# Attention of a two-layer trunk: one group of steps per unit, latent values for both sample tiles at once, and TensorE's mixers in the order of the source

## The chip, the cores and the metric

The kernel runs on one core of a Trainium2 chip. The metric is the device time of one execution in microseconds (us); it was run three times. Engines: TensorE (PE; its weight loads are listed as PEld), VectorE (DVE), ScalarE (ACT), GpSimd (POOL) and SyncE (SP), whose queue starts most transfers.

## The reference

Two layers of a trunk for 128 prompt tokens and 256 sample tokens, which share all weights (fp32, width 1024). In each layer three mixers read the same normalised input; a merge of them goes through one output projection; a squared-ReLU MLP follows.

```python
h = rms(x) * (1 + sc1) + sh1                     # shift, scale, gate from the condition
u_conv, dq, dk, dv, cq, ckv, kpe, gl = split(h @ w_in)
o_conv = silu(rms(dwconv31(a * sigmoid(gate)))) @ w_conv_out
# differential: 4 heads, two 64-wide halves each, values 128 wide
q, k = rms64(dq), rms64(dk)                      # sample: 2-d rope, 128 cached keys in front
w = softmax(q1 k1 / 8) - lam * softmax(q2 k2 / 8)
o_diff = (rms128(w @ v) * (1 - lam_init)) @ w_diff_out
# latent: 8 heads, 96-wide queries and keys, values 64 wide
qm = rms96(rms(cq) @ w_uq);  k_nope, vm = split(rms(ckv) @ w_ukv)
km = rms96(k_nope ++ kpe)                        # rope on the last 32; cached ckv, kpe in front
o_mla = (softmax(qm km / sqrt(96)) @ vm) @ w_mla_out
x = x + g1 * ((s0 * o_conv + s1 * o_diff + s2 * o_mla) @ w_out)      # s = sigmoid(gl)
x = x + g2 * (relu(h2 @ w_up) ** 2 @ w_down)
```

The prompt attends to its own 128 keys; the sample to 128 cached and its own 256, 384 together.

## The kernel before

**Tokens and projections.** The 384 tokens are three tiles of 128 (tile 0 the prompt, tiles 1 and 2 the sample). Activations lie feature-major, 128 channels by 384 tokens. Every fp32 product with a weight is made from rounded parts: `split` (L194, L195) cuts a weight into a rounded `wh` (ScalarE) and the rest `wl` (VectorE), and `passes` (L201 to L203) issues three matmuls. A weight buffer comes free when its last matmul has run; `wh` has four, `wl` three, and the raw pieces `wr` four. The loads go through SyncE's queue in the order of use.

**The main line and its side lines.** `mixers` runs `weave(dense, chains, attention)`. `dense` is the main generator: the projections for differential attention (`qkv`), the compressed latents (`cproj`), the convolution's input (`conv_in`), the latent queries (`mla_q`) and keys and values (`mla_kv`, weights `ukv`), the gates (`gate`), and the output projections of the branches (`branch_out`). In layer 0 it also has units of the modulation matmul (`mod_unit`), whose transposes run some units later through `after`. It yields the weight of each step in units: 1 is three passes of 384 columns, 0.667 a step of 256 columns.

The side generators yield either the name of a flag that they wait for, or a number of units, from the table `W`, after which their next steps are put in between. `chains` holds, in this order, the transposes of differential queries and keys (`qkv_T`, L653), the norms of the latents (`cproj_norms`), the transposes of latent queries (L921) and keys (L936) in `mla_T`, and the norm of the convolution (`conv_norm`). `attention` holds two groups of two heads of differential attention and two groups of four heads of latent attention.

**Attention.** A unit of differential attention is a token tile and a head. `softmax2` (L755) makes the scores of the two halves into two PSUM banks, VectorE the maximum, ScalarE the exponential, and L808 combines the halves into one weight matrix; `weightsT` (L770) transposes it, ScalarE copies it to `eT`, and L822 multiplies it with the values. When all units of a pair of heads are done, a reciprocal square root of ten small VectorE operations (`rsqrt`, L305 to L316), a scaling and `to_fm` (L780) bring the output to feature-major. Scores of the next unit, transposes of this one and its values are three steps, with `W["s"]`, `W["t"]` and so on between them. A unit of latent attention is a token tile and two heads, 64 rows of the output each: L967 issues for each block of 128 keys one matmul per head, the two side by side in the array's columns. The two sample tiles are separate units, each with 128-column matmuls.

**Order on the engines.** The kernel is written in Tile, whose planner orders the instructions of each engine beforehand. Every instruction has a priority by its place in the source; the planner takes the first in that order whose operands it expects to be there, and so steps over a late one. Weight loads and splits are 400 places ahead (`high_priority(AHEAD)`). This also holds for TensorE in the mixers; only layer 0's first norm is written out by hand (`manual_schedule`, where the engines named keep the order of the source). The convolution is 31 taps on VectorE for each of four channel blocks (L1024, 240 of the longer form in all); their place in the source is late, after the last gate, so they fill VectorE wherever nothing before them is ready.

**PSUM.** Eight banks: three for projections (`mm`), two for scores (`sc`), one for the transposes of `chains` and the norms (`tw`), one for those of attention (`ta`), one for values (`av`).

Of the kernel before, what the change touches and what calls it, by code (L numbers as in the profile page):

```python
# [21 lines left out]
P = 128  # L22
# [111 lines left out]
W = {"rm": 9, "rx": 8.5, "c0": 3.5, "c1": 2, "qh": 2, "mh": 5.5, "qT": 12.5, "kT": 20, "s0": 3.5, "s": 4.5, "t": 3, "od": 9, "mq": 7.5, "mk": 11.5, "ms": 7.5, "mt": 0.5, "ma": 2, "bc": 11}  # L134
ENGINES = {mybir.EngineType.PE, mybir.EngineType.Activation, mybir.EngineType.DVE}
SLOT = {"ot": 848, "z": 400, "tmp": 400, "tmpA": 400, "x": 512}
# [4 lines left out]
PBANKS = {"mm": 3, "sc": 2, "tw": 1, "ta": 1, "av": 1}  # L141
# [3 lines left out]
class Body:  # L145
# [19 lines left out]
    def slot(self, tag, w=T, dt=F32):  # L165

        t = (self.xp if tag == "x" else self.hp).tile([P, SLOT.get(tag, T)], dt, tag=tag, name=self.nm(tag), bufs=SLOTS[tag])
        return t[:, :w]
# [75 lines left out]
    def tick(self, w):  # L244
        for e in self.todo:
            e[0] -= w
        while self.todo and self.todo[0][0] <= 0:
            self.todo.pop(0)[1]()

    def weave(self, main, *sides):  # L250
# [17 lines left out]
        for w in main:  # L268
# [4 lines left out]
            self.tick(w)  # L273
            for e in list(st):
                e[1] -= w
                while e in st and e[1] <= 0 and step(e):
                    pass
                e[1] = max(e[1], 0) if e[2] else e[1]
# [38 lines left out]
    def rstd_bc(self, acc, toks, ahead=0):  # L317

        V = self.V
        st = self.psum("tw")  # L320
# [11 lines left out]
        bc = self.psum("tw")  # L332
# [22 lines left out]
    def mod_unit(self, l, s, p, pool=None):  # L355
# [11 lines left out]
        def rest():  # L367
            pt = self.psum("tw")
# [11 lines left out]
        self.after(4, rest)  # L380
# [137 lines left out]
    def layer_consts(self, l):  # L518
# [26 lines left out]
        pr = self.tl(self.cp, [P, 2, 64], "lpr")  # L545
# [91 lines left out]
    def qkv_T(self, l, c):  # L637
# [3 lines left out]
        for i in range(2):  # L641
# [8 lines left out]
            for hh in range(2):  # L650
                pt = self.psum("tw")
# [8 lines left out]
                yield W["qh"]  # L660
# [28 lines left out]
    def cproj_norms(self, l):  # L689
# [5 lines left out]
        st = self.psum("tw")  # L695
# [71 lines left out]
    def weightsT(self, e, n):  # L767
        pt = self.psum("ta")
# [6 lines left out]
    def to_fm(self, o, gain):  # L775

        V, A, E = self.V, self.A, self.E
        pt = self.psum("ta")
# [8 lines left out]
    def diff_attention(self, c):  # L787
# [23 lines left out]
        e = scores(*units[0])  # L811
        yield W["s0"]
        for i, (tt, hd) in enumerate(units):
            nxt = scores(*units[i + 1]) if i + 1 < len(units) else None
            yield W["s"]
            k0, n = (0, P) if tt == 0 else (P, T)
            wT = self.weightsT(e, n)
            yield W["t"]
# [5 lines left out]
            e = nxt  # L824
            if hd == 0:
                continue
# [7 lines left out]
            V.tensor_tensor(m2, m2, q, ALU.add)  # L834
        y = self.rsqrt(ms, 2 * NT)
# [9 lines left out]
        for k in range(2):  # L845
            self.od.append(self.to_fm(o[:, k], self.sub))
            yield 2
# [61 lines left out]
    def mla_T(self, l, g):  # L909
# [8 lines left out]
        for hh in range(4):  # L918
            pt = self.psum("tw")
# [4 lines left out]
            if hh < 3:  # L924
                yield W["mh"]
# [4 lines left out]
        for pr in range(2):  # L930
            kT = self.tl(self.ap, [P, 2, NK], "kT", 3)
            for i in range(2):
                hh = 2 * pr + i
                pt = self.psum("tw")
                for tt in range(4):
                    E.transpose(pt[0:96, tt * P : tt * P + P], m["ks"][tt // 2][:, tt % 2, hh, :], self.ident)  # L936
                A.activation(kT[0:96, i, :], pt[0:96, :], AF.Identity,
                             scale=self.pv[l][0:96, PV["mk"][0] : PV["mk"][1]])
                yield W["mh"]
# [3 lines left out]
    def mla_attention(self, g):  # L943
# [3 lines left out]
        for pr, (qT, kT) in enumerate(pairs):  # L947
            for tt in range(NT):
                k0, n = (0, P) if tt == 0 else (P, T)
                s1 = self.tl(self.ap, [P, 2], "ms1", 2)  # L950
                es = self.softmax2([qT[0:96, i, :] for i in range(2)], [kT[0:96, i, :] for i in range(2)],
                                   tt, k0, n, qsc[:, 4 * tt + 2 * pr : 4 * tt + 2 * pr + 2], s1)
                r = self.tl(self.ap, [P, 2], "mr", 2)
                V.reciprocal(r, s1)
                for i in range(2):
                    V.tensor_scalar(es[i][:, :n], es[i][:, :n], r[:, i : i + 1], None, op0=ALU.mult)
                yield W["ms"]
                eT = []
                for i in range(2):
                    eT.append(self.weightsT(es[i], n))  # L960
                    yield W["mt"] if i == 0 else W["ma"]
                if tt == 0:
                    av = self.psum("av")
                for j in range(n // P):
                    for i in range(2):
# [455 lines left out]
```

## Time and profile before

| | |
|---|---|
| median of 3 runs | 1368.37 us (1367.15 to 1368.58) |
| the profiled execution | 1366.81 us |
| its span | 1365.0 us |
| TensorE clock granted, mean | 0.999 of full speed |
| busy, share of the span | PE 99%, PEld 93%, DVE 78%, ACT 50%, POOL 1% |
| DMA | 209.46 MB, mean 153 GB/s |

The span runs from the first to the last instruction; the profiled execution's time is 1.8 us longer. Busy shares are averages over stages with different limits. A matmul's bar in the timeline overlaps the next one's, so the time that one takes from the others is read from the distances between starts. A name like `mm<-wh,h` is the output tile and the operands by the program's names; `128*128 128x384` is the stationary operand and the moving one.

### The profile page before, as it was taken

Reading aid. Unit: us, or ns where it says so; the run is one execution under the profiler, and the core shown is the slowest. Engines: PE = TensorE matmul, PEld = TensorE weight load, DVE = VectorE, ACT = ScalarE, POOL = GpSimd, SP = SyncE. Lnnn points to the kernel's source line nnn. Section 1 sums busy time; section 2 is a strip of 40 time slices with the busy share of each in tenths; the row PEclk is TensorE's granted clock in tenths of the full one; section 3 lists DMA queues with packets and bytes.
Section 4 is the critical chain, followed back from the end, with each engine's and each line's share of the span. In section 5 each row is a group of like instructions: output and inputs, shape, how many; then the busy total and the mean of one; then the engine's idle time right before and its main releaser. Section 6 shows DMA issues by size and latency. Waiting matters only on the chain.

```text
span 1365.0 us, 22037 instructions
## 1 busy us (share of the span) xinstructions
PE 1346.7 (99%) x8192; PEld 1263.6 (93%) x8192; DVE 1065.2 (78%) x2549; ACT 686.8 (50%) x1297; POOL 16.7 (1%) x34
## 2 busy tenths in 40 slices
PE   5999999999999999999999999999999999999998
PEld 3999887879999999999999999988899999999998
DVE  5777998995998999974568779989999897435532
ACT  3556656443544662276346566664544456326621
POOL 0000000000000000000000000000000000000000
PEclk9999999999999999999999999999999999999999
DMA  9533344445574667753544323222257454333341
GB/s 364 180 95 108 122 141 146 139 173 214 157 256 128 206 220 244 248 162 124 150 145 138 105 88 106 92 80 89 79 198 254 149 180 160 124 124 124 124 147 54
DMA packets 62683, 209.46 MB, mean 153 GB/s; under 512 B 7840, under 2 KB 13600, under 8 KB 62320
## 3 DMA queue, kind: packets, MB, share of 16 engines
q1 hardware_dynamic: 56304, 196.93, 43.9%
q0 software_dynamic: 1808, 6.63, 1.5%
q10 hardware_dynamic: 4464, 4.50, 0.9%
q8 instruction: 64, 1.05, 0.3%
q14 instruction: 43, 0.35, 0.1%
HBM read 203.54 MB, written 4.49 MB: 152 GB/s over the span
## 4 chain that ended last, share of the span: by engine, by line
PE 96%; DVE 2%; DMA 1%; ACT 1%; SPq 0%; issue 0%; DVEq 0%
PE mm L201 20%; PE mm L202 19%; PE mm L203 19%; PE sc L201 9%; PE sc L203 9%; PE sc L202 9%; PE sc L755 3%; PE av L967 2%; PE ta L770 2%; PE mm L362 1%; DMA wr<-wts 1%; PE av L822 1%; PE tw L936 1%; PE tw L921 0%; DVE wl L195 0%; PE tw L653 0%
## 5 line engine op out<-in xcount | busy, mean ns | idle before, releaser
L194 ACT CAST wh<-wr 128x1024 fp32r<-128x1024 f32 (+3 forms) x280 | 289.7, 1036 | 343.2 <-PE mm L202 168.7
L195 DVE TENSOR_TENSOR wl<-wr,wh 128x1024 fp32r<-128x1024 f32 (+3 forms) x280 | 336.5, 1203 | 153.8 <-PE mm L203 63.7
L201 PE MATMUL mm<-h,wh 128*128 128x384 f32 x848 | 292.9, 346 | 0.5 <-ACT wh L194 0.5
L203 PE MATMUL mm<-h,wl 128*128 128x384 f32 x848 | 285.6, 337 | 0.6 <-DVE wl L195 0.6
L202 PE MATMUL mm<-h,wh 128*128 128x384 f32 x592 | 199.9, 338 | 0.2 <-DVE h L435 0.2
L201 PEld LDWEIGHTS mm<-h,wh 128*128 128x128 f32 x848 | 159.6, 188 | 10.6 <-issue 7.2
L203 PEld LDWEIGHTS mm<-h,wl 128*128 128x128 f32 x848 | 159.4, 188 | 1.5 <-DVE wl L195 1.0
L1024 DVE SCALAR_TENSOR_TENSOR z<-u,dwh,z 128x399 f32<-128x399 f32 x240 | 146.9, 627 | 0.3
L390 DVE SCALAR_TENSOR_TENSOR ot<-wm,srow 128x1024 bf16<-128x1024 f32 x112 | 136.5, 1219 | 3.5 <-DMA wm<-modwT 2.9
L202 PEld LDWEIGHTS mm<-h,wh 128*128 128x128 f32 x592 | 111.4, 188 | 1.8 <-DVE h L435 0.6
L203 PE MATMUL sc<-h,wl 128*128 128x384 f32 x336 | 112.4, 335 | 0.0
L201 PE MATMUL sc<-h,wh 128*128 128x384 f32 x336 | 112.3, 334 | 0.0
L202 PE MATMUL mm<-o,wh 128*128 128x384 f32 x320 | 107.9, 337 | 0.0
L201 PE MATMUL mm<-x,wh 128*128 128x386 f32 x288 | 98.2, 341 | 0.0
L203 PE MATMUL mm<-x,wl 128*128 128x386 f32 x288 | 97.6, 339 | 0.0
L202 PE MATMUL mm<-x,wh 128*128 128x386 f32 x288 | 97.5, 339 | 0.0
L201 PE MATMUL sc<-x,wh 128*128 128x386 f32 x272 | 92.6, 340 | 0.0
L203 PE MATMUL sc<-x,wl 128*128 128x386 f32 x272 | 92.1, 339 | 0.0
L202 PE MATMUL sc<-x,wh 128*128 128x386 f32 x272 | 92.1, 339 | 0.0
L1302 ACT ACTIVATE tmp<-tmp 128x128 f32<-128x128 f32 (+1 forms) x128 | 51.6, 448 | 69.1 <-DVE tmp L1300 68.9
L201 PE MATMUL mm<-wh,h 128*128 128x256 f32 (+1 forms) x288 | 85.0, 295 | 0.0
L202 PE MATMUL mm<-wl,h 128*128 128x256 f32 (+1 forms) x288 | 82.0, 285 | 0.0
(267 smaller groups left out, 2644.3 us busy)
## 6 DMA issues: line engine op xcount, KB each, us to landing
wr<-wts SPq DMA_DIRECT2D x306, 512.0 KB, 3.5
wm<-modwT SPq DMA_DIRECT2D x56, 512.0 KB, 4.1
srow<-condrow POOLq DMA_DIRECT2D x2, 1024.0 KB, 7.4
wr<-wts SPq DMA_DIRECT2D x4, 432.0 KB, 3.4
G<-xT SPq DMA_DIRECT2D x8, 192.0 KB, 4.5
wr<-wts SPq DMA_DIRECT2D x4, 384.0 KB, 3.1
G<-xT POOLq DMA_DIRECT2D x8, 192.0 KB, 3.5
xd<-G ACTq DMA_DIRECT2D x8, 192.0 KB, 2.2
```

The source lines that it names most:

```text
L194: self.A.copy(hi[:, :n], w[:, :n])
L195: self.V.tensor_tensor(lo[:, :n], w[:, :n], hi[:, :n].bitcast(F32), ALU.subtract)
L201: self.E.matmul(ps, ah, bh, start=start, stop=False)
L202: self.E.matmul(ps, ah, bl, start=False, stop=False)
L203: self.E.matmul(ps, al, bh, start=False, stop=stop)
L362: E.matmul(ps[32 * j : 32 * j + 32, :256], self.cond[:, 4 * h + j, :], w[:, j * 256 : j * 256 + 256], start=h == 0, stop=h == 1, tile_posi ...
L390: V.scalar_tensor_tensor(j, w, 0.5, self.srow[:, c, :], ALU.mult, ALU.mult, accum_out=self.modT[l][:, b, c : c + 1])
L755: E.matmul(sc[:, :n], q[c][:, qs], k[c][:, ks], start=True, stop=True)
L770: self.E.transpose(pt[:, j : j + P], e[:, j : j + P], self.ident)
L967: E.matmul(av[64 * i : 64 * i + 64, tt * P : tt * P + P], vm[:, k0 // P + j, hv : hv + 64], eT[i][:, j * P : j * P + P], start=j == 0, sto ...
L1024: self.V.scalar_tensor_tensor(z[b], self.u[:, b, k : k + ZW], self.dw[:, b * CK + k : b * CK + k + 1], z[b], ALU.mult, ALU.add)
L1302: A.activation(r[:, s:e], r[:, s:e], AF.Relu, bias=r[:, T + c : T + c + 1])
```

## The change

The change touches the mixers of both layers.

- The weave of the mixers stands in `manual_schedule(engines={PE})`: TensorE runs its instructions there in the order of the source. The other engines stay with the planner.
- Differential attention has one group of steps per unit: scores of the next unit, transposes of this one, values of the one before; then `W["s"]` = 7 units. Both `to_fm` of a pair of heads stand together, as do the two heads of `qkv_T` and pairs of heads in `mla_T` (`mh` 11 after every second head).
- Latent attention has one group per unit as well: transposes of this unit, scores of the next, values of the one before; then `W["ms"]` = 9.5. The two sample tiles share `eT`, 768 columns wide, ordered by key block and then tile, and their values are one matmul of 256 columns per key block and head.
- `weave` and `tick`: when a side line's step is due, side steps that would be due within `NEAR` = 2 units, and steps of `after` due within 7, are put with it. Modulation transposes come 14 units after their matmul instead of 4.
- `tw` and `ta` become one tag `tr` with two banks. `eT` moves to the pool of the mixers, the `lpr` constant into a slot of `tmp`.

The diff, without the renamed PSUM tags; the old body of `mla_attention` stands above in the code.

```diff
@@ -131,14 +131,16 @@
 PIECE = 1024


-W = {"rm": 9, "rx": 8.5, "c0": 3.5, "c1": 2, "qh": 2, "mh": 5.5, "qT": 12.5, "kT": 20, "s0": 3.5, "s": 4.5, "t": 3, "od": 9, "mq": 7.5, "mk": 11.5, "ms": 7.5, "mt": 0.5, "ma": 2, "bc": 11}
+W = {"rm": 9, "rx": 8.5, "c0": 3.5, "c1": 2, "mh": 11, "qT": 12.5, "kT": 20, "s": 7, "od": 9, "mq": 7.5, "mk": 11.5, "ms": 9.5, "bc": 11}
+
+NEAR = 2
 ENGINES = {mybir.EngineType.PE, mybir.EngineType.Activation, mybir.EngineType.DVE}
-SLOT = {"ot": 848, "z": 400, "tmp": 400, "tmpA": 400, "x": 512}
+SLOT = {"ot": 848, "z": 400, "tmp": 400, "tmpA": 400, "x": 512, "eT": 768}
 AHEAD = 400


 SLOTS = {"h": 16, "z": 5, "ot": 1, "o": 12, "cq": 10, "G": 15, "tmp": 4, "tmpA": 3, "e": 3, "eT": 2, "x": 16}
-PBANKS = {"mm": 3, "sc": 2, "tw": 1, "ta": 1, "av": 1}
+PBANKS = {"mm": 3, "sc": 2, "tr": 2, "av": 1}
 TE = T + 2


@@ -241,10 +244,10 @@

         self.todo.append([n, f])

-    def tick(self, w):
+    def tick(self, w, due=False):
         for e in self.todo:
             e[0] -= w
-        while self.todo and self.todo[0][0] <= 0:
+        while self.todo and self.todo[0][0] <= (7 if due else 0):
             self.todo.pop(0)[1]()

     def weave(self, main, *sides):
@@ -270,10 +273,12 @@
                 while w not in self.flags:
                     assert any([step(e) for e in list(st)]), (w, [e[2] for e in st])
                 continue
-            self.tick(w)
+            for e in st:
+                e[1] -= w
+            due = any(e[1] <= 0 and not (e[2] and e[2] not in self.flags) for e in st)
+            self.tick(w, due)
             for e in list(st):
-                e[1] -= w
-                while e in st and e[1] <= 0 and step(e):
+                while e in st and e[1] <= (NEAR if due else 0) and step(e):
                     pass
                 e[1] = max(e[1], 0) if e[2] else e[1]
         while st:
...
@@ -377,7 +382,7 @@

         if pool:
             return rest
-        self.after(4, rest)
+        self.after(14, rest)

     def mod_block(self, l, b):

...
@@ -808,22 +812,16 @@
             V.scalar_tensor_tensor(es[0][:, :n], es[1][:, :n], ra, es[0][:, :n], ALU.mult, ALU.add)
             return es[0]

-        e = scores(*units[0])
-        yield W["s0"]
-        for i, (tt, hd) in enumerate(units):
-            nxt = scores(*units[i + 1]) if i + 1 < len(units) else None
-            yield W["s"]
+        def values(tt, hd, wT):
+            nonlocal av
             k0, n = (0, P) if tt == 0 else (P, T)
-            wT = self.weightsT(e, n)
-            yield W["t"]
             if hd == 0:
                 av = self.psum("av")
             for j in range(n // P):
                 E.matmul(av[:, hd * P : hd * P + P], wT[:, j * P : j * P + P],
                          v[:, k0 // P + j, hd * P : hd * P + P], start=j == 0, stop=j == n // P - 1)
-            e = nxt
             if hd == 0:
-                continue
+                return
             s1 = st[tt]
             a3 = av[:, :256].rearrange("p (h e) -> p h e", h=2)
             A.copy(o[:, :, tt, :], a3)
@@ -832,6 +830,18 @@
             q = self.tl(self.ap, [P, 2], "oss", 2)
             V.scalar_tensor_tensor(q, s1[:, :, 0], EPS, s1[:, :, 0], ALU.mult, ALU.mult)
             V.tensor_tensor(m2, m2, q, ALU.add)
+
+
+        e, last = scores(*units[0]), None
+        yield W["s"]
+        for i, u in enumerate(units):
+            nxt = scores(*units[i + 1]) if i + 1 < len(units) else None
+            wT = self.weightsT(e, P if u[0] == 0 else T)
+            if last:
+                values(*last)
+            e, last = nxt, (*u, wT)
+            yield W["s"]
+        values(*last)
         y = self.rsqrt(ms, 2 * NT)
         for k in range(2):
             for tt in range(NT):
@@ -844,7 +854,6 @@
         yield W["od"]
         for k in range(2):
             self.od.append(self.to_fm(o[:, k], self.sub))
-            yield 2
         self.flags.add(f"od{c}")

     def mla_q(self, l, g):
...
@@ -916,12 +925,12 @@
         yield W["mq"]
         qs = [self.tl(self.ap, [P, 2, T], "qT", 3) for _ in range(2)]
         for hh in range(4):
-            pt = self.psum("tw")
+            pt = self.psum("tr")
             for tt in range(NT):
                 E.transpose(pt[0:96, tt * P : tt * P + P], m["x4"][:, tt, hh, :], self.ident)
             A.activation(qs[hh // 2][0:96, hh % 2, :], pt[0:96, :T], AF.Identity,
                          scale=self.pv[l][0:96, PV["mq"][0] : PV["mq"][1]])
-            if hh < 3:
+            if hh == 1:
                 yield W["mh"]
         self.flags.add(f"mqT{g}")
         yield f"mk{g}"
@@ -931,11 +940,12 @@
             kT = self.tl(self.ap, [P, 2, NK], "kT", 3)
             for i in range(2):
                 hh = 2 * pr + i
-                pt = self.psum("tw")
+                pt = self.psum("tr")
                 for tt in range(4):
                     E.transpose(pt[0:96, tt * P : tt * P + P], m["ks"][tt // 2][:, tt % 2, hh, :], self.ident)
                 A.activation(kT[0:96, i, :], pt[0:96, :], AF.Identity,
                              scale=self.pv[l][0:96, PV["mk"][0] : PV["mk"][1]])
+            if pr == 0:
                 yield W["mh"]
             m["pairs"].append((qs[pr], kT))
         self.flags.add(f"mkT{g}")
@@ -944,38 +954,75 @@
         V, A, E = self.V, self.A, self.E
         yield f"mkT{g}"
         pairs, vm, qsc = (self.m[g][n] for n in ("pairs", "vm", "qsc"))
...
+        units = [(pr, tt) for pr in range(2) for tt in range(NT)]
+        av, eT = None, None
+
+        def scores(pr, tt):
+            qT, kT = pairs[pr]
+            k0, n = (0, P) if tt == 0 else (P, T)
+            s1 = self.tl(self.ap, [P, 2], "ms1", 2)
+            es = self.softmax2([qT[0:96, i, :] for i in range(2)], [kT[0:96, i, :] for i in range(2)],
+                               tt, k0, n, qsc[:, 4 * tt + 2 * pr : 4 * tt + 2 * pr + 2], s1)
+            r = self.tl(self.ap, [P, 2], "mr", 2)
+            V.reciprocal(r, s1)
+            for i in range(2):
+                V.tensor_scalar(es[i][:, :n], es[i][:, :n], r[:, i : i + 1], None, op0=ALU.mult)
+            return es
+
+        def weights(tt, es):
+
+            nonlocal eT
+            if tt < 2:
+                eT = [self.slot("eT", 2 * T) for _ in range(2)]
+            n = 1 if tt == 0 else NT
+            for i in range(2):
+                pt = self.psum("tr")
+                for j in range(n):
+                    E.transpose(pt[:, j * P : j * P + P], es[i][:, j * P : j * P + P], self.ident)
+                if tt == 0:
+                    A.copy(eT[i][:, :P], pt[:, :P])
+                else:
+                    A.copy(eT[i].rearrange("p (j t q) -> p t j q", j=NT, t=2)[:, tt - 1],
+                           pt[:, :T].rearrange("p (j q) -> p j q", j=NT))
+
+        def values(pr, tt, eT):
+            nonlocal av
+            if tt == 0:
+                av = self.psum("av")
+            n, q0, w = (1, 0, P) if tt == 0 else (NT, P, NS)
+            for j in range(n):
                 for i in range(2):
...
+                    hv = (2 * pr + i) * 64
+                    E.matmul(av[64 * i : 64 * i + 64, q0 : q0 + w], vm[:, (j + 1) if tt else 0, hv : hv + 64],
+                             eT[i][:, j * w : j * w + w], start=j == 0, stop=j == n - 1, tile_position=(0, 64 * i))
+
+        def out(pr):
             hi, lo = self.slot("o", T, F32R), self.slot("o", T, F32R)
             A.copy(hi, av[:, :T])
             V.tensor_tensor(lo, av[:, :T], hi.bitcast(F32), ALU.subtract)
             self.om.append((hi, lo))
             self.flags.add(f"m{2 * g + pr}")
...
+
+
+        es, last, done = scores(*units[0]), None, None
+        yield W["ms"]
+        for i, (pr, tt) in enumerate(units):
+            if done is not None:
+                if g == 1:
+                    yield "od"
+                out(done)
+                done = None
+            weights(tt, es)
+            es = scores(*units[i + 1]) if i + 1 < len(units) else None
+            if last:
+                values(*last)
+                done = last[0] if last[1] else None
+            last = (pr, tt, eT) if tt != 1 else None
+            yield W["ms"]
+        values(*last)
+        yield 2
+        out(1)
+        yield 0.5
         self.flags.add(f"om{g}")

     def conv_in(self, l, b, act, rstd=None):
@@ -1166,7 +1213,8 @@
         self.d, self.m = [{}, {}], [{}, {}]
         self.od, self.om, self.oc = [], [], []
         m = []
-        self.weave(self.dense(l, h, m), self.chains(l), self.attention())
+        with self.tc.manual_schedule(engines={mybir.EngineType.PE}):
+            self.weave(self.dense(l, h, m), self.chains(l), self.attention())
         ap.close()
         self.xs = ExitStack()
         self.xp = self.xs.enter_context(self.tc.tile_pool(name=f"xp{l}", bufs=1))
```

## Rows read from the trace of the kernel before

**Rows 1.** Sections 1 and 4 of the page: engine totals, chain's shares.

```profile
PE 1346.7 (99%) x8192; PEld 1263.6 (93%) x8192; DVE 1065.2 (78%) x2549; ACT 686.8 (50%) x1297; POOL 16.7 (1%) x34
...
PE 96%; DVE 2%; DMA 1%; ACT 1%; SPq 0%; issue 0%; DVEq 0%
```

**Rows 2.** Waits of TensorE: tile and line, released by; total us, times, longest.

```profile
PE tw L322 <- DVE z L344: 10.9, 1, 10.9
PE av L362 <- DMA wr<-wts: 1.0, 1, 1.0
```

**Rows 3.** Windows: stretch, length, busy by engine (PE PEld DVE ACT POOL), PEclk, DMA.

```profile
49.60:366.00 316.40, 316.29 (x2092) 276.68 (x2091) 265.92 (x770) 171.67 (x377) 3.27 (x6) 1.00 0.43 142
...
826.00:995.00 169.00, 168.83 (x988) 145.71 (x987) 158.80 (x422) 95.48 (x205) 0.55 (x1) 1.00 0.29 95
```

**Rows 4.** Timeline of PE, latent values: start us, us, engine line operation out<-in xcount.

```profile
923.77 0.34 PE L203 MATMUL mm<-o,wl 128*128 128x384 f32 x1
924.04 0.89 PE L967 MATMUL av<-eT,v 128*64 128x128 f32 x12
...
961.93 0.43 PE L967 MATMUL av<-eT,v 128*64 128x128 f32 x2
...
963.38 0.87 PE L967 MATMUL av<-eT,v 128*64 128x128 f32 x10
```

**Rows 5.** Timeline of PE, three transposes between projections.

```profile
746.30 0.28 PE L203 MATMUL mm<-wh,h 128*128 128x256 f32 x1
746.42 0.49 PE L653 MATMUL tw<-ident,tok 128*128 128x128 f32 x3
746.87 0.28 PE L202 MATMUL mm<-wl,h 128*128 128x256 f32 x1
```

**Rows 6.** Timeline of PE, scores of two units of differential attention.

```profile
770.91 0.92 PE L755 MATMUL sc<-kT,qT 64*128 64x384 f32 x4
...
776.25 1.56 PE L755 MATMUL sc<-kT,qT 64*128 64x384 f32 x4
```

**Rows 7.** Timeline of PE, last ukv matmul and transposes of latent keys.

```profile
182.32 0.39 PE L203 MATMUL mm<-wh,ccl 128*128 128x512 f32 x1
...
183.23 0.33 PE L203 MATMUL mm<-h,wl 128*128 128x384 f32 x1
183.40 0.34 PE L201 MATMUL mm<-h,wh 128*128 128x384 f32 x1
...
193.30 0.38 PE L936 MATMUL tw<-ident,tok 128*96 128x128 f32 x2
...
198.99 0.42 PE L936 MATMUL tw<-ident,tok 128*96 128x128 f32 x2
```

**Rows 8.** Timeline of DVE, reciprocal square root and convolution taps.

```profile
188.72 0.16 DVE L310 TENSOR_TENSOR nwa<-nwy 128x8 f32<-128x8 f32 x1
188.79 0.62 DVE L1024 SCALAR_TENSOR_TENSOR z<-u,dwh,z 128x399 f32<-128x399 f32 x1
189.34 0.15 DVE L311 TENSOR_TENSOR nwa<-nwa,kmss 128x8 f32<-128x8 f32 x1
...
195.95 0.96 DVE L195 TENSOR_TENSOR wl<-wr,wh 128x768 fp32r<-128x768 f32 x1
```

**Rows 9.** Timeline of PE, transposes of latent queries.

```profile
169.32 0.51 PE L921 MATMUL tw<-ident,tok 128*96 128x128 f32 x2
...
171.26 0.27 PE L921 MATMUL tw<-ident,tok 128*96 128x128 f32 x1
```

**Rows 10.** Timeline of PE, last values and first transposes of differential outputs.

```profile
164.97 0.83 PE L822 MATMUL av<-v,eT 128*128 128x128 f32 x6
...
179.60 0.33 PE L780 MATMUL ta<-ident,ot 128*128 128x128 f32 x1
```

**Rows 11.** Timelines of PE and DVE, from scores to softmax result.

```profile
836.23 0.92 PE L755 MATMUL sc<-kT,qT 64*128 64x384 f32 x4
...
843.39 0.61 DVE L808 SCALAR_TENSOR_TENSOR e<-e,ra,e 128x384 f32<-128x384 f32 x1
```

More of the change, by code (lines that the diff above doesn't have):

```diff
@@ L165, in slot @@
     def slot(self, tag, w=T, dt=F32):
-        t = (self.xp if tag == "x" else self.hp).tile([P, SLOT.get(tag, T)], dt, tag=tag, name=self.nm(tag), bufs=SLOTS[tag])
+        pool = self.xp if tag == "x" else self.ap if tag == "eT" else self.hp
+        t = pool.tile([P, SLOT.get(tag, T)], dt, tag=tag, name=self.nm(tag), bufs=SLOTS[tag])
         return t[:, :w]
@@ L319, in rstd_bc @@
         V = self.V
-        st = self.psum("tw")
+        st = self.psum("tr")
         for i, o in enumerate(toks):
@@ L331, in rstd_bc @@
         yield W["bc"]
-        bc = self.psum("tw")
+        bc = self.psum("tr")
         self.E.matmul(bc[:, :T], self.ones, dg, start=True, stop=True)
@@ L544, in layer_consts @@
         lp = r("lam").rearrange("p (f d) -> p f d", f=4)
-        pr = self.tl(self.cp, [P, 2, 64], "lpr")
+        pr = self.slot("tmp", 128).rearrange("p (f d) -> p f d", f=2)
         V.tensor_tensor(pr, lp[:, 0:4:2, :], lp[:, 1:4:2, :], ALU.mult)
@@ L659, in qkv_T @@
                     A.copy(dst[:, hh, 0:T], pt[:, :T])
-                yield W["qh"]
         self.flags.add(f"kT{c}")
@@ L693, in cproj_norms @@
         yield W["c0"]
-        st = self.psum("tw")
+        st = self.psum("tr")
         for i in range(NT):
@@ L767, in weightsT @@
     def weightsT(self, e, n):
-        pt = self.psum("ta")
+        pt = self.psum("tr")
         for j in range(0, n, P):
@@ L777, in to_fm @@
         V, A, E = self.V, self.A, self.E
-        pt = self.psum("ta")
+        pt = self.psum("tr")
         for tt in range(NT):
@@ L918, in mla_T @@
         for hh in range(4):
-            pt = self.psum("tw")
+            pt = self.psum("tr")
             for tt in range(NT):
@@ L933, in mla_T @@
                 hh = 2 * pr + i
-                pt = self.psum("tw")
+                pt = self.psum("tr")
                 for tt in range(4):
@@ L946, in mla_attention @@
         pairs, vm, qsc = (self.m[g][n] for n in ("pairs", "vm", "qsc"))
[L947 to L954, printed above, removed]
-                for i in range(2):
[L956 to L965, printed above, removed]
-                        hv = (2 * pr + i) * 64
-                        E.matmul(av[64 * i : 64 * i + 64, tt * P : tt * P + P], vm[:, k0 // P + j, hv : hv + 64],
-                                 eT[i][:, j * P : j * P + P], start=j == 0, stop=j == n // P - 1,
-                                 tile_position=(0, 64 * i))
-            yield 2
-            if g == 1:
-                yield "od"
@@ new lines, in weights @@
+        def weights(tt, es):
[4 more added lines that the diff above has]
+            for i in range(2):
+                pt = self.psum("tr")
+                for j in range(n):
[5 more added lines that the diff above has]
+                           pt[:, :T].rearrange("p (j q) -> p j q", j=NT))
@@ L977, in mla_attention @@
             self.flags.add(f"m{2 * g + pr}")
-            yield 0.5
+        es, last, done = scores(*units[0]), None, None
[17 more added lines that the diff above has]
+        yield 0.5
         self.flags.add(f"om{g}")
```

## The prediction

> **What bounds the kernel now.** I read the engine totals and the chain on the page first. TensorE is busy 1346.7 of 1365.0 us and carries 96% of the chain [rows 1], so a change pays only if it shortens TensorE's own sequence. The waits of TensorE come next: the longest is 10.9 us at the very start, before the first weights [rows 2], and the whole run's list has nothing above 1.1 us behind it. TensorE never stands still in the mixers, because an operand that is late is stepped over: the planner, which is free to order TensorE, puts projection matmuls in front of it. The windows show that layer 0's mixers take 316 us at full clock, and that in layer 1, from 826 to 995 us, VectorE is busy 158.8 of 169 us [rows 3]. So what TensorE gets from VectorE there arrives late. That makes two questions: what do the small matmuls cost, and how late are the operands at the place where the source asks for them?
>
> Busy times say little about the first, as a matmul's bar overlaps the next one. I go by distances between starts.
>
> **The change part by part.**
>
> *Latent values at once (gains).* A latent unit's values are 12 records: three key blocks, two heads side by side, two records per fp32 matmul. Run whole they last 0.89 us; cut by the planner into 2 and 10 they last 0.43 and 0.87 [rows 4]. Each cut adds an entry and an exit of about 0.1 us: 923.77 to 924.04 is 0.27 where two projection matmuls stand 0.17 apart [rows 4, 7]. So a cut unit costs 1.30 + 0.2 = 1.5 us. 14 of the 16 units of sample tiles are cut, two run whole: 14 x 1.5 + 2 x 0.89 = 22.8 us. Afterwards 8 groups serve both tiles with 12 records of 256 columns. I take twice the column time: of 0.89 us some 0.6 us is columns, so 1.2 + 0.3 = 1.5 us a group, 12 us in all. Gain 10.8 us. Nothing shows a 256-column record of this shape; if it took no longer than 128 columns the gain would be 16, at 2.5 times 8.5. The prompt tile (4 records, in 7 of 8 cases cut into 2 and 2, 2 x 0.43 + 0.2 = 1.1 us) becomes one lump of 0.5: 4 us more. Taken: 15 us, bounds 10 to 20.
>
> *Fewer, larger groups of steps.* Does a break of the projections cost anything? Three transposes between projections move the projection from 746.30 to 746.87, 0.57 us, of which two steps of 0.12 are its own: 0.33 us for three, 0.11 each [rows 5], as they run in a row. A break by transposes is free, so putting steps together (the `due`/`NEAR` lines, `qh`, `mh`, `od`) gains nothing; 0 taken, at most the 0.1 us switch of a column- or row-split matmul. What grouping can gain is in the scores: the two 64-row halves run side by side in 0.92 us, but 1.56 us where the second half's bank is late [rows 6]. 4 of 16 such units are like this, two by 0.65 and two by about 1 us: 3 us. With some 2 us of small holes the planner left, gains are **20 us**; bounds 10 (values alone, low) to 25.
>
> *TensorE in the order of the source (losses).* Whoever is late now holds everything behind him: the projections, and with them the release of weight buffers. So each late operand is priced by its lateness against its place in the source. A unit of `W` is three projection matmuls, 3 x 0.17 = 0.52 us [rows 7].
>
> (a) Transposes of the latent keys, L936. Their place is 11.5 units after the last `ukv` matmul; that number stays. Layer 0, first half of the heads: last `ukv` start 182.32, so the place is 182.55 + 6.0 + 0.33 for three transposes in between = 188.9. The trace has the first two transposes at 193.30 and the third at 198.99 [rows 7]. The reason is on VectorE: the reciprocal square root is a chain of ten 0.16 us operations, and after each one a convolution tap of 0.62 us slips in before the next is ready, so that L310 to L311 is 0.62 apart [rows 8]; the keys themselves (L903) are done just ahead of 198.99. At 188.9 that chain has barely begun. A standing TensorE frees no weight buffers, so the two weight splits in the rest of it (the longer is 0.96 [rows 8], the other about half) fall away: 10.0 - 1.4, a wait of 8.6 us. There are four such places. By the same count: layer 1 first 868.0 against 876.5, 7 us after the discount; the second ones have an attention group of about 2.6 us in between and come to 3 and 5. Sum 24. Lower bound, if no tap were issued: ten operations back to back and the rest, about 5.6 us after `ukv`, that is no wait, 0. Upper bound without discount, 28.
>
> (b) Transposes of the latent queries, first half: the third token tile comes at 171.26 instead of 169.32 [rows 9], 3.0 us in layer 1. Taken 4 for both; 0 to 5.
>
> (c) Differential outputs of the second pair of heads: place 9 units after the values, 165.6 + 4.7 + 0.7 of transposes + 1.9 from (b) = 172.9; the trace has it at 179.60 [rows 10]. 6.7 us, 5 after the discount, layer 1 3: taken 8, 0 to 11. The first pair meets no taps and is on time.
>
> (d) Softmax. Source distance from scores to the transposes of their result falls from 12 units to 7. In the last unit of a pair there is room for 0.92 + 0.33 + 0.67 + 3.65 = 5.6 us, and the chain took 836.23 to 844.00, 7.8 us [rows 11]. Units before it have 0.92 more room. Four last units at 1.5 and twelve middle ones near 0: 6, bounds 0 to 14. Latent softmax has 9.5 units instead of 7.5; 3 us, 0 to 10.
>
> (e) One shared ring of two PSUM banks for all transposes, and the norm's broadcast (11 units, conv_norm's comes 13 to 14 units late): 3 us, 0 to 8. The first waits for ScalarE's copies.
>
> Sum of waits 48. A wait of 5 to 8 us also lets VectorE get through taps that would have delayed the next chain, and taps come in a fixed number; I take a fifth off: **38 us**, bounds 8 (only half of (a) and nothing else stays, a third of it made good) to 60.
>
> *What costs nothing:* the DMAs are unchanged in number and order on SP's queue, which loads ahead of need and waits for buffers only; `eT` and `lpr` only change their place in SBUF; ScalarE's strided copies have the same elements, on an engine at 50% [rows 1]. A mod unit's transposes come up to 14 units after it; they are read much later.
>
> Net: 38 - 20 = 18 us on a run of 1366.81 us (span 1365.0 and 1.8 us around it): **1385 us**. That run is 1.6 us under the median of those shown, well inside what follows.
>
> The Trainium skill, "TensorE: Matmul & The Clock Gate", Part 3 (The mechanism), says that weight loads may be pulled ahead while matmuls start and end in program order. By that rule nothing behind a late transpose can start, which is what (a) to (d) assume; the trace of before has no late operand in its order that would show it.
>
> **Rivals.**
> 1. *The waits are short, and the change is faster.* Mechanism: once TensorE stands, no new weights are split and no results come for VectorE to evacuate, so only taps compete with the chains; if those are mostly run before or after the chains, (a) shrinks to its bare 5.6 us and vanishes. Place: L936, L780, L921. It decides when all waits together fall under 20 us. For it: VectorE keeps 10 us idle in 826 to 995 [rows 3]. Against: ten taps between ten small operations are in the rows for both layers [rows 8]. Time: 20 us gained, 0 to 17 lost: 1347 to 1363, middle 1353.
> 2. *Both sides cancel:* waits of 18 to 22 us, 1364 to 1371.
> 3. *The order costs more than its waits.* The clock was 1.00 in all of the mixers [rows 3], where no stop occurs; with four stops of 3 to 8 us TensorE may come back at the lower of its two levels. If each is followed by some 6 us of it, half of that is lost, 4 x 3 = 12 us beside the forecast, more if the smaller waits do the same: 1398 to 1415. The Trainium skill, "TensorE: Matmul & The Clock Gate", HAM oscillation, warns that idle gaps bring the clock back to half; no run here shows it in the mixers.
> 4. *The change doesn't do what it says:* projections emitted after the region (gate 0) fill the waits. Only possible near the end, for conv_norm, at most 2 us; no case of its own.
>
> **How the numbers follow.** Forecast (slower, 1371 to 1404) 0.50, rival 3 0.10, rival 2 0.09, rival 1 0.31, rival 4 inside the forecast. A difference under 0.2% (2.7 us) can't be told from none. Slower is 0.61, with 0.01 from rival 2's edge, same 0.08, faster 0.31. The range takes in rival 1 but for its best end, down to 1349, and goes up to 1404, which leaves some 0.06 below and 0.06 above, from rival 3. The likeliest case alone is 1371 to 1404.
>
> **What would show it.** Values: records with 256 columns, 12 in a row, some 1.5 us; transposes still 0.11 apart. (a): idle time of TensorE in front of L936, put down to DVE `tok` L903, 15 to 30 us in sum; (c) the same at L780 from `ot`; (b) at L921; (d) at L770 from `e` L808. The waits of TensorE should go from 15 to over 40 us. If L936 shows under 5 us, the forecast is wrong in its main term, and rival 1 holds; if TensorE's waits are as forecast and the span still falls, the values were worth more than 20. Clock under 1.00 in slices after the waits speaks for rival 3.

## The result and the profile after

The changed kernel takes 1432.64 us (median of 4, 1429.63 to 1437.63) against 1368.34 us: ratio 1.0479 (95% interval 1.0465 to 1.0494), 64 us slower. The direction was forecast, the size was not: 1385 us, with a range up to 1404. Lines have moved; L204 to L206 are now the three matmuls of `passes`, L945 the transposes of latent keys, L981 those of latent weights, L996 the latent values.

The engine totals, the clock in 40 slices and the chain's shares of the page, to be read against [rows 1]:

```profile
PE 1349.6 (94%) x8096; PEld 1273.9 (89%) x8096; DVE 1075.2 (75%) x2549; ACT 688.8 (48%) x1297; POOL 16.7 (1%) x34
...
PEclk9999989899999999999999999898999999999999
...
PE 82%; DVE 13%; ACT 3%; issue 1%; DMA 1%; SPq 1%; DVEq 0%; ACTq 0%
```

TensorE is busy as long as before (some of it now at half clock), but the span has grown, VectorE has 13% of the chain instead of 2%, and the clock falls in slices of the two mixers only. The waits of TensorE (beside [rows 2]; total us, times, longest):

```profile
PE tr L945 <- DVE tok L912: 22.3, 5, 5.8
PE tr L327 <- DVE z L349: 10.9, 1, 10.9
PE tr L981 <- DVE e L969: 7.6, 5, 2.3
PE tr L774 <- DVE e L812: 7.0, 6, 2.1
PE tr L784 <- DVE ot L851: 4.1, 1, 4.1
PE tr L981 <- DVE nwa L318: 3.8, 1, 3.8
PE tr L338 <- DVE tmp L334: 3.7, 2, 1.9
PE tr L930 <- DVE tok L585: 3.0, 1, 3.0
PE tr L981 <- ACT qT L931: 2.6, 1, 2.6
```

The same two stretches as in [rows 3]: TensorE stands for 28 and 27 us of them, and the clock is 0.96 and 0.92 on the mean.

```profile
49.60:366.00 316.40, 288.23 (x1865) 250.82 (x1864) 241.96 (x702) 156.19 (x348) 1.10 (x2) 0.96 0.39 128
826.00:995.00 169.00, 142.15 (x789) 125.66 (x788) 153.81 (x432) 88.45 (x198) 0.00 (x0) 0.92 0.24 76
```

One stop from near, layer 0's first latent keys. The timeline of TensorE, to be read against [rows 7]; in brackets the idle time ahead and what ended it:

```profile
199.75 0.33 PE L205 MATMUL mm<-h,wh 128*128 128x384 f32 x1
199.92 0.34 PE L206 MATMUL mm<-h,wl 128*128 128x384 f32 x1
200.10 0.38 PE L945 MATMUL tr<-ident,tok 128*96 128x128 f32 x2
206.01 1.52 PE L945 MATMUL tr<-ident,tok 128*96 128x128 f32 x6 [5.54 <-DVE tok L912]
...
207.65 0.52 PE L205 MATMUL mm<-h,wh 128*128 128x384 f32 x1
207.97 0.52 PE L206 MATMUL mm<-h,wl 128*128 128x384 f32 x1
```

VectorE in that stop goes on as in [rows 8]; a tap stands between any two steps of the reciprocal square root:

```profile
201.84 0.16 DVE L315 TENSOR_TENSOR nwa<-nwy 128x8 f32<-128x8 f32 x1
201.91 0.63 DVE L1071 SCALAR_TENSOR_TENSOR z<-u,dwh,z 128x399 f32<-128x399 f32 x1
202.46 0.16 DVE L316 TENSOR_TENSOR nwa<-nwa,kmss 128x8 f32<-128x8 f32 x1
```

And windows through it: the granted clock falls to the lower of its two levels while TensorE stands, and stays there for 4.9 us of work. Projections are then 0.32 us apart (207.65 to 207.97) where they were 0.17 apart.

```profile
200.50:204.10 3.60, 0.00 (x0) 0.00 (x0) 3.60 (x13) 0.29 (x1) 0.00 (x0) 1.00 0.51 148
204.10:206.00 1.90, 0.00 (x0) 0.00 (x0) 1.90 (x6) 0.00 (x0) 0.00 (x0) 0.50 0.00 0
206.00:210.90 4.90, 4.88 (x18) 4.81 (x18) 4.90 (x10) 1.37 (x2) 0.00 (x0) 0.50 0.01 3
210.90:215.00 4.10, 4.10 (x38) 3.15 (x37) 3.43 (x9) 1.17 (x3) 0.00 (x0) 1.00 0.48 140
```

**An account of TensorE's sequence.** From its first to its last matmul in the profiled execution three things add up: idle time, what the half clock takes (half of the busy time spent at that level), and the rest, the work at full clock. Each is worked out from the whole timeline and the clock in it (us); the medians are of all executions, so they differ by up to 4.2 us from the one that was profiled:

| kernel | median | idle | half clock | work |
|---|---|---|---|---|
| before | 1368.3 | 3.8 | 1.7 | 1344.9 |
| changed | 1432.6 | 65.4 | 24.4 | 1325.2 |
| e1 planner's order | 1354.3 | 8.1 | 3.2 | 1328.9 |
| e2 before, strict order | 1464.2 | 83.4 | 31.2 | 1336.0 |
| e3 three taps of 31 | 1398.2 | 41.5 | 16.3 | 1323.7 |
| e4 fillers | 1425.1 | 46.7 | 17.5 | 1344.3 |
| e5 prompt's eT | 1430.4 | 64.3 | 28.2 | 1325.8 |
| e6 e1 with that eT | 1356.6 | 6.9 | 1.5 | 1331.5 |
| e7 `ms` 13 | 1443.8 | 69.9 | 34.7 | 1324.2 |
| e8 before, merged values | 1364.2 | 4.7 | 1.6 | 1342.0 |
| e9 e1, values cut | 1355.3 | 6.5 | 1.6 | 1330.6 |
| e10 e1 without `NEAR` | 1360.4 | 11.5 | 3.2 | 1330.7 |
| e11 later keys, layer 0 | 1431.3 | 63.7 | 29.9 | 1323.7 |
| e12 `mk` 16.5 | 1423.0 | 56.9 | 24.7 | 1325.1 |

So the change is +61.6 idle, +22.7 half clock, -19.7 work: 64.6 us.

### The profile page after: what moved, and what is told of

It reads as the page before. It is cut to its first block, busy times and chain, and to the rows that moved or that the text cites. A ratio compares the mean times of both kernels' runs of the same rounds, so it can differ in the third digit from the quotient of the medians.

```text
span 1429.6 us, 21854 instructions
## 1 busy us (share of the span) xinstructions
PE 1349.6 (94%) x8096; PEld 1273.9 (89%) x8096; DVE 1075.2 (75%) x2549; ACT 688.8 (48%) x1297; POOL 16.7 (1%) x34
## 4 chain that ended last, share of the span: by engine, by line
PE 82%; DVE 13%; ACT 3%; issue 1%; DMA 1%; SPq 1%; DVEq 0%; ACTq 0%
PE mm L204 16%; PE mm L205 16%; PE mm L206 16%; PE sc L204 8%; PE sc L206 8%; PE sc L205 8%; DVE z L1071 3%; DVE wl L198 3%; PE sc L759 2%; DMA wr<-wts 1%; PE av L996 1%; ACT e L766 1%; PE tr L981 1%; PE mm L367 1%; PE tr L945 1%
## 5 line engine op out<-in xcount | busy, mean ns | idle before, releaser
L204 PE MATMUL mm<-h,wh 128*128 128x384 f32 x848 | 293.3, 346 | 0.5 <-ACT wh L197 0.5
L206 PE MATMUL mm<-h,wl 128*128 128x384 f32 x848 | 286.6, 338 | 0.6 <-DVE wl L198 0.6
L204 PEld LDWEIGHTS mm<-h,wh 128*128 128x128 f32 x848 | 162.3, 191 | 5.7 <-issue 3.0
L206 PEld LDWEIGHTS mm<-h,wl 128*128 128x128 f32 x848 | 161.7, 191 | 1.0 <-DVE wl L198 1.0
L205 PEld LDWEIGHTS mm<-h,wh 128*128 128x128 f32 x592 | 114.0, 193 | 1.2 <-DVE h L440 0.8
L206 PE MATMUL sc<-h,wl 128*128 128x384 f32 x336 | 112.3, 334 | 0.0
L204 PE MATMUL sc<-h,wh 128*128 128x384 f32 x336 | 112.2, 334 | 0.0
L204 PE MATMUL mm<-x,wh 128*128 128x386 f32 x288 | 98.1, 341 | 0.0
L206 PE MATMUL mm<-x,wl 128*128 128x386 f32 x288 | 97.5, 339 | 0.0
L204 PE MATMUL sc<-x,wh 128*128 128x386 f32 x272 | 92.5, 340 | 0.0
L206 PE MATMUL sc<-x,wl 128*128 128x386 f32 x272 | 92.1, 338 | 0.0
L204 PE MATMUL mm<-wh,h 128*128 128x256 f32 (+1 forms) x288 | 85.4, 297 | 0.0
L206 PE MATMUL mm<-wh,h 128*128 128x256 f32 (+1 forms) x288 | 83.6, 290 | 0.3 <-DVE h L440 0.3
```

Of the source, the lines that this page charges most:

```text
L204: self.E.matmul(ps, ah, bh, start=start, stop=False)
L205: self.E.matmul(ps, ah, bl, start=False, stop=False)
L206: self.E.matmul(ps, al, bh, start=False, stop=stop)
```

## Experiments

**e1, e2: the order alone.** e1 is the changed kernel without the added `with` line; e2 is the kernel before with it.

```diff
-        with self.tc.manual_schedule(engines={mybir.EngineType.PE}):
-            self.weave(self.dense(l, h, m), self.chains(l), self.attention())
+        self.weave(self.dense(l, h, m), self.chains(l), self.attention())
```

> The changed kernel with its mixers handed back to the planner: only the order written out by hand for TensorE is taken away; groups, merged latent values, PSUM ring and distances stay. Theory (the order makes waits of 61.6 us and half-clock stretches that cost 22.7 us, while the rest of the change saves 19.7 us of TensorE's work): TensorE's idle time falls to under 6 us, no half clock in the mixers, and the time is 1348 us (1343 to 1355), faster than before. Rival 1 (the groups, the shared PSUM ring or the longer distances are what costs): it stays above 1400. Rival 2 (the saving comes only because a strict order keeps groups whole; the planner cuts them again): no waits, but 1360 to 1368.

> The kernel before with one edit: TensorE in the mixers strictly in the order of the source. Theory (the order alone is the cost): waits at the transposes of latent keys (L936), of latent weights and of softmax results, 50 to 110 us in sum, half-clock stretches after them, less some 10 us as values and scores are no longer cut: 1410 to 1480, middle 1435. Rival (the regrouped steps and their distances make the waits, the order is harmless with the old steps): within 1360 to 1385.

e1: 1354.29 us, ratio to before 0.9907 (0.9892 to 0.9922). e2: 1464.15 us, 1.0707 (1.0686 to 1.0729). The order is the whole loss: it costs 78 us with the new steps and 97 us with the old ones. The rest of the change is a gain of 13 us under the planner's order (31 us in the strict one), and e1 beats both kernels, the one before by 0.9%. e1 came 6 us above the middle of its range: the work is 3.7 us longer than in strict order (1328.9 for 1325.2), as the planner still cuts some groups, and 8.1 us of idle time are left where under 6 were expected; the mixers have no half clock, as expected. In e2 the largest waits sit at the transposes of softmax weights (L770: 30.9 us in all):

```profile
PE ta L770 <- DVE e L956: 18.0, 12, 3.9
...
PE ta L770 <- ACT eT L772: 7.7, 14, 0.8
```

All of it belongs to latent attention, where the old steps leave 7.5 units in place of 9.5. Differential attention, where they leave more, has no wait there.

**e3: fewer convolution taps.** 28 of 31 taps are left out.

```diff
-            for k in range(1, CK):
+            for k in range(1, 3):
```

> The changed kernel with 2 further convolution taps per channel block in place of 30 (28 of 31 taps are left out, some 140 us of VectorE's work). Theory (the late operands are late because a tap slips in after each small operation of the chains on VectorE): idle time in front of the transposes of latent keys (L945) falls from 22.3 us to under 6, of TensorE in all from 65 to under 35, half-clock stretches to a third: 1365 to 1395, middle 1380. Rival (the chains are too long for their distances even with VectorE to themselves): L945 keeps over 15 us and the time stays above 1410.

1398.19 us. Idle time at L945 went from 22.3 to 3.8 us, so the taps are what makes the keys late. But the other waits stayed: TensorE's idle time is 41.5 us where under 35 were expected, and the half clock takes 16.3 where a third of 24.4 was. Waits of TensorE:

```profile
PE tr L774 <- DVE e L812: 7.0, 6, 2.1
PE tr L981 <- DVE e L969: 6.8, 4, 3.4
PE tr L945 <- DVE tok L912: 3.8, 3, 1.4
PE tr L338 <- DVE tmp L334: 3.7, 2, 1.9
PE tr L784 <- DVE ot L851: 3.5, 1, 3.5
```

The softmax waits stay with most taps gone (L774 as before, L981 at 14.1 us for 17.0), so they are not mainly the taps' doing; the time came 3 us above the range for that.

**e4: work where TensorE stands.**

```diff
                 pt = self.psum("tr")
+                for _ in range(40 if hh == 0 else 0):
+                    E.transpose(pt[:, 0:P], self.ident, self.ident)
```

> The changed kernel with 40 extra transposes of a constant (some 4.4 us) in front of the first transposes of latent keys, at the four places where TensorE stands for 4.8 to 5.8 us: work is added where it stands idle, nothing is taken away. Theory (the half clock behind these stops costs time of its own): idle time at L945 falls to under 9 us, the four half-clock stretches of 6.8 us behind them go, and the time falls by 8 to 10 us, to 1423. Rival (the half clock costs nothing, as what comes after the stop waits for VectorE anyway): 1430 to 1435. Rival (fillers delay the transposes): above 1436.

1425.09 us (1423.03 to 1427.45), 7.5 us less with 160 transposes more. The stop above is filled (TensorE's timeline):

```profile
200.70 4.53 PE L945 MATMUL tr<-ident 128*128 128x128 f32 x40
205.06 0.38 PE L947 MATMUL tr<-ident,tok 128*96 128x128 f32 x2
206.61 0.86 PE L947 MATMUL tr<-ident,tok 128*96 128x128 f32 x6 [1.17 <-DVE tok L912]
...
207.49 0.34 PE L205 MATMUL mm<-h,wh 128*128 128x384 f32 x1
207.66 0.34 PE L206 MATMUL mm<-h,wl 128*128 128x384 f32 x1
```

The keys come no sooner (206.61), but the projections behind them are 0.17 apart at once. The half clock's loss fell by 6.9 us, about what the time did. Of the four stretches three are gone; the fourth, behind a stop of 2.0 us that is left, is half as long.

**e5, e6: the ring of two `eT`.** ScalarE's copies to `eT` waited 17.6 us for values that stand behind them in TensorE's order (waits of ScalarE in the changed kernel):

```profile
ACT eT L985 <- PE av L996: 17.6, 7, 4.7
```

Left out of the diff are the three smaller tiles that make room.

```diff
...
-                eT = [self.slot("eT", 2 * T) for _ in range(2)]
+                eT = [self.slot("eT", 2 * T) if tt else self.tl(self.ap, [P, P], "eTp", 2) for _ in range(2)]
```

> The changed kernel, still in strict order, with the prompt's two transposed weight tiles of each latent group in small buffers of their own, so that the sample's pair no longer waits for the prompt's values (three constants' tiles are cut to the size used to make room). In the changed kernel ScalarE waits 17.6 us in 7 places with a copy to eT (L985) for the values (L996) that stand behind it in TensorE's order, and everything behind that copy on ScalarE waits too. Theory (that ring of two is behind half of the 17.0 us of idle time at the latent transposes L981): ScalarE's wait falls under 4 us, L981 to under 10 us, time 1432 to some 1421. Rival (the softmax chain is too long for 9.5 units, whatever ScalarE's copies do): L981 stays above 14 us, time within 3 us of the changed kernel's.

> The same buffers in the kernel whose TensorE order is the planner's (1354.3 us). Theory (the planner steps over what waits, so the ring costs it cuts at most): 1352 to 1355, no difference that can be told. Rival (the ring cuts groups there and costs TensorE's work): 1347 to 1351.

e5: 1430.37 us; those waits of ScalarE are gone and L981 still stands 16.3 us. The theory falls and the rival holds: an earlier copy made nothing else earlier. e6: 1356.56 us (1355.00 to 1357.69), 1.6 us above its range and no gain either.

**e7, e11, e12: distances.** e7 sets `"ms": 13`, e12 `"mk": 16.5`. e11:

```diff
-            if i == (2 if l == 0 else 3):
+            if i == 3:
                 yield from self.mla_kv(l, 1)
```

> The changed kernel in strict order with 13 units in place of 9.5 between a latent unit's scores and its transposes. Theory of the ring: L981 keeps more than 11 of its 17 us, time 1425 to 1440. Rival (distance): L981 falls under 8 us, time 1415 to 1425.

> The changed kernel in strict order with the second latent group's keys and values in layer 0 one gate (16 units) later, as they already are in layer 1; then nothing in layer 0 is forced: in the changed kernel its main line waits there for the flag mqT1 and the side lines run their steps with no projections between. Theory (the latent transposes L981 wait most where steps are forced): the 2.6 us gap ahead of the last forced unit of layer 0 goes, L981 falls from 17.0 to 12 to 15 us while layer 1's gaps of 2.3 and 3.8 us stay; time 1424 to 1431. Rival (the softmax chain is too long for the distance anywhere): L981 stays at 16 to 18 us, 1430 to 1436.

> The changed kernel in strict order with 16.5 units in place of 11.5 between a latent group's keys and their transposes. Theory (the distances have no room left: what one chain gains, later steps lose, as they are forced): idle time at the key transposes L945 falls from 22.3 us to 10 to 15, at the latent transposes L981 it rises from 17.0 to over 23, and the time stays within 1425 to 1440. Rival (the distances were only set too short, and the strict order can be mended by them): 1405 to 1420.

e7: 1443.77 us, outside both ranges, and L981 rose to 24.1 us, where one theory had it above 11 and the other under 8. TensorE's timeline in layer 1 of the changed kernel shows why (projections left out; there are none behind 963.06):

```profile
956.99 1.46 PE L759 MATMUL sc<-kT,qT 96*128 96x384 f32 x4
958.37 1.51 PE L996 MATMUL av<-eT,v 128*64 128x256 f32 x12
963.06 0.85 PE L981 MATMUL tr<-ident,e 128*128 128x128 f32 x6 [2.28 <-DVE e L969]
963.74 1.46 PE L759 MATMUL sc<-kT,qT 96*128 96x384 f32 x4
965.13 0.44 PE L996 MATMUL av<-eT,v 128*64 128x128 f32 x4
969.38 1.51 PE L981 MATMUL tr<-ident,e 128*128 128x128 f32 x6 [3.81 <-DVE nwa L318]
```

The main line has reached `mla_kv` of the second group, which waits for the flag `mqT1`; that needs the first pair of heads of the first group, so the side lines' steps are forced, with no unit between scores and transposes. Longer distances push more steps into such places (another is the flag `om1`). In e7:

```profile
PE tr L981 <- DVE e L969: 22.8, 7, 4.3
```

In all seven the timeline has no projection between a unit's scores and its transposes; the other units, with 8 units or more between, wait 1.3 us in sum. Counted in the same way in the changed kernel, the forced units (4, 1.3 and 0 projection units between) make 8.7 of the 17.0 us at L981. The other 8.4 us, in seven units of 0.4 to 1.7 us each, stand behind 5 to 10 units: there the distance itself is too short. So e7's second theory holds for these, and what it gained there was lost in forced places. e11 takes layer 0's forced steps away: L981 14.0 as expected, the 2.6 us gap down to 0.3. Yet the time is unchanged (1431.32): L945 stands 24.3 and the half clock takes 29.9. e12: 1422.97 us; L945 12.2, L981 20.2. Neither range holds, and both theories are half right: of 10.1 us taken off the keys 3.2 came back at L981, where three forced units now make 11.1 us, and the rest stayed won, mending the order a little.

**e8, e9, e10: what the gain is made of.** e8 is the kernel before with one wide `eT` for both sample tiles and one 256-column matmul per key block and head. e9 is e1 with these matmuls cut; e10 is e1 with `tick(w, False)` and `e[1] <= 0` in place of the rule with `NEAR`.

e8 (the lines that fill the wide `eT` are left out), and below it e9:

```diff
...
+                if tt == 1:
+                    continue
...
+                q0, w = (0, P) if tt == 0 else (P, NS)
...
+                        E.matmul(av[64 * i : 64 * i + 64, q0 : q0 + w], vm[:, (j + 1) if tt else 0, hv : hv + 64],
+                                 eT[i][:, j * w : j * w + w], start=j == 0, stop=j == n // P - 1,
...
```

```diff
+            for t in range(0, w, P):
...
-                    E.matmul(av[64 * i : 64 * i + 64, q0 : q0 + w], vm[:, (j + 1) if tt else 0, hv : hv + 64],
-                             eT[i][:, j * w : j * w + w], start=j == 0, stop=j == n - 1, tile_position=(0, 64 * i))
+                        E.matmul(av[64 * i : 64 * i + 64, q0 + t : q0 + t + P], vm[:, (j + 1) if tt else 0, hv : hv + 64],
+                                 eT[i][:, j * w + t : j * w + t + P], start=j == 0, stop=j == n - 1, tile_position=(0, 64 * i))
```

> The kernel before with one part of the change: both sample tiles in one eT and their latent values in one 256-column matmul; steps, distances, PSUM tags and the planner's order as before. Theory (the merged values are nearly all of what the change saves under the planner's order, 13 us; the regrouped steps give nothing): 1352 to 1358. Rival (grouping gives half of it): 1359 to 1364.

> The kernel with the changed steps and the planner's order (1354.3 us), with the latent values of the two sample tiles cut again into 24 matmuls of 128 columns, all 24 in one group; all else stays. Theory (what the change saves under the planner's order is groups that stay whole, since both copies of the weights are there before the values start; the 256-column form itself saves 8 groups x (2 x 0.89 - 1.51) = 2 us): 1354 to 1359. Rival (the 256-column matmul is the saving): 1361 to 1366.

> The same kernel (planner's order, changed steps) without the rule that puts side steps due within 2 units, and modulation transposes due within 7, together with a step that is due. Theory of the prediction (putting steps together saves nothing, as a break of the projections is free): within 1 us of 1354.3. Rival (140 breaks in place of 202 are part of the saving): 1356 to 1361.

e8: 1364.21 us, above its range and 0.2 us above the rival's: only 4 us gained. The planner still cuts all eight sample groups; e1 has them whole but one. TensorE's timelines, first e8, then e1:

```profile
904.59 0.65 PE L978 MATMUL av<-eT,v 128*64 128x256 f32 x2
905.63 1.51 PE L978 MATMUL av<-eT,v 128*64 128x256 f32 x10
```

```profile
913.05 1.52 PE L996 MATMUL av<-eT,v 128*64 128x256 f32 x12
```

e9: 1355.30 us, not to be told from e1. From start to next start, the latent value matmuls take 23.3 us before, 21.6 in e8, 16.7 in e9 and 15.4 in e1: whole groups give 6.6, the wider matmul 1.3, the entries into the groups not counted. That they are whole because a group stands one step behind its transposes, with both copies there, was not tried by itself. e10: 1360.36 us, 6 us more: under the planner's order the rule does pay. In the profiled executions idle time is 11.5 for 8.1 us and the work 1.8 us longer. Of the idle time 1.8 us is one stop (waits of TensorE):

```profile
PE mm L204 <- ACT tok L870: 1.8, 1, 1.8
```

So what a break of the projections costs by itself is not shown, nor what the rule is worth in strict order.

## Why the prediction was wrong

The direction was right, at a chance of 0.61, and the mechanism of (a) too. Net, 18 us were forecast and 64 measured. Of the 46 us missed the half clock is 22.7, latent softmax in (d) 14, and the fifth taken off the waits 10; the other differences nearly cancel.

*Gains: 20 forecast, 19.7 found,* but in part from elsewhere, so the agreement is luck. The values' 15 is near: from start to next start at full clock the latent values take 23.3 us before and 14.5 in the changed kernel, and the entries, which the prediction counts and which lie in the distances ahead of the groups, are 45 before and 16 now, at some 0.12 us each. That is 12.5 us together. One group takes 1.51 us, as worked out. The scores, put at 3, are 42.9 and 42.8 us, now with most of the entries in them. The rest was not in the forecast: projections take 13.4 us less (some 2 of them entries), differential values 3.0 and the modulation 1.7 less, while all transposes take 7.5 us more. The `NEAR` rule, put at 0, is worth 6 under the planner's order (e10). So whether a break by three transposes is free [rows 5] stays open.

*(a), (b), (c) stood.* Latent keys 24 forecast, 22.3 found, and by the mechanism named (e3). The single stops, forecast at 8.6, 3, 7 and 5, are 5.5, 4.8, 6.2 (in two pieces) and 5.8, so the sum is nearer than its parts. Latent queries 4 and 3.9; differential outputs 8 and 4.4, as layer 1's part did not come; (e) 3 and 3.9, at the norm's broadcast (L338).

*(d) failed in its size.* Differential softmax 6 forecast, 7.9 found; latent softmax 3 forecast, without a working of its own, and 17.0 found. The step took 9.5 units for granted and enough. It did not follow the main line to the flag `mqT1`, where next to nothing stands between (8.7 us), and it did not set the length of the chain against the distance elsewhere (8.4 us).

*The fifth taken off* was to come from a standing TensorE that lets VectorE get through its taps. The sum shows none of it: waits came to 61.6 us where 48, less the fifth 38, were taken.

*The half clock was left out of the forecast,* and stood as rival 3, with a chance of 0.10 and 12 us. It takes 24.4 us, 22.7 more than before. Behind the four long stops it is 9.9 us, near the rival's 12; the rest lies behind stops of 1.2 to 4.1 us. e4 shows that its price is real time. The prediction had the clock from the mixers alone; the trace of before has such a stretch near its start, behind the 1.03 us wait for a weight (TensorE's timeline, then a window):

```profile
20.35 0.87 PE L362 MATMUL av<-wr,cond 128*32 128x256 f32 x8 [1.03 <-DMA wr<-wts]
...
20.65:24.00 3.35, 3.35 (x27) 0.87 (x20) 1.84 (x7) 1.60 (x5) 0.00 (x0) 0.50 1.02 418
```

The Trainium skill, "TensorE: Matmul & The Clock Gate", HAM oscillation, warns that idle gaps cost the clock as well as the time they last; the windows above bear that out.

38 became 61.6 + 22.7, less 19.7 of work: 64.6. That is above rival 3 as well, which had the waits too small.

## What to carry to other kernels

Where a planner steps over late operands, a trace without waits says nothing about how late they are. Before fixing an engine's order, count for each operand the work that stands between its maker and its user, also where the main line forces the side lines. A stop of some 5 us on TensorE cost its own length and 2 to 3 us more here, for what ran behind it at the lower clock. Groups that stay whole gave more here than the wider matmul did.

## What had not been expected of the hardware

Of two kernels the one with 160 transposes more, in a place where TensorE stood, was faster by 7.5 us. Short stops had the lower clock behind them too. In the changed kernel the shortest such stop lasted 1.18 us (L774 at 810.03 us; windows through it and behind it):

```profile
810.00:811.20 1.20, 0.03 (x1) 0.00 (x0) 1.14 (x3) 0.00 (x0) 0.00 (x0) 1.00 0.73 287
...
811.65:815.05 3.40, 3.40 (x18) 3.40 (x18) 1.74 (x6) 2.25 (x8) 0.00 (x0) 0.50 0.00 0
```

Behind one of 2.06 us, also at L774, it was the same:

```profile
829.30:831.30 2.00, 0.04 (x1) 0.00 (x0) 1.71 (x5) 2.00 (x6) 0.00 (x0) 1.00 0.25 25
831.30:832.10 0.80, 0.69 (x7) 0.73 (x8) 0.38 (x2) 0.06 (x1) 0.00 (x0) 1.00 0.54 184
832.10:835.50 3.40, 3.40 (x17) 3.40 (x16) 0.19 (x1) 0.85 (x2) 0.00 (x0) 0.51 0.38 140
```

Another stop of 1.18 us at 95.07 us and the one of 2.28 us at 960.8 us have full clock behind them, and what tells them apart is left open.
